# Second norm inside the first gate product, token halves right behind it, 17 pairs by seven, first weight sums in Mamba, down projection behind the last pair

## The chip, the cores and the metric

The kernel runs on one NeuronCore of a Trainium2 chip. The engines that matter are TensorE (PE, matrix products, with its weight loads shown as PEld), VectorE (DVE), ScalarE (ACT), GpSimd (POOL, here almost only for issuing transfers) and SyncE (SP, which issues most loads). Each engine works through its own instructions in order. The metric is the device time of one execution in microseconds. The kernel before was timed three times: 873.16, 873.23 and 875.12 us, median 873.23.

## The reference

The computed layer takes 512 positions of width 1024, with 16 learned positions put ahead of them, in float32. A normalised input goes through one projection to two mixers, their outputs through one output projection, and a gated MLP follows:

```python
def conv_glu_ffn(h, w_up, conv_w, conv_b, w_down):
    u = causal_dwconv(h @ w_up, conv_w, conv_b)
    gate, val = jnp.split(u, 2, axis=-1)
    return (jax.nn.silu(gate) * val) @ w_down

def reference(...):
    h = jnp.concatenate([meta, x], axis=1)
    for l in range(DEPTH):
        u = rmsnorm(h, norm1_w[l])
        proj = u @ w_in[l]
        hg_q, hg_f, hg_i, hg_g, m2_z, m2_xbc, m2_dt = jnp.split(proj, PROJ_SPLITS, axis=-1)
        out_a = hgrn2_mixer(hg_q, hg_f, hg_i, hg_g, lbs[l], hg_norm_w[l])
        out_b = mamba2_mixer(m2_z, m2_xbc, m2_dt, ...)
        h = h + jnp.concatenate([out_a, out_b], axis=-1) @ w_out[l]
        h = h + conv_glu_ffn(rmsnorm(h, norm2_w[l]), ...)
    return rmsnorm(h, final_norm_w)[:, N_META:, :]
```

`rmsnorm` divides by the root of the mean square over the 1024 channels. `w_up` is 1024 x 5632: 2816 gate columns and 2816 value columns. `causal_dwconv` is a convolution of width 3 along the positions, per channel.

## The kernel before

Channels lie on the 128 partitions, positions along the free dimension (528, of which the MLP needs 514). Each float32 operand of a product is split in a high and a low half of a format that TensorE takes (`F32R`), and each product is three matmuls: high by high, high by low, low by high. A weight block of 128 x 1024 is loaded by SP (`raw`), copied by ACT into the high half (`whi`, line 182) and subtracted by DVE for the low half (`wlo`, line 183). There are three buffers of each kind, and blocks are asked for two ahead of their use (`weights`, `ahead`).

The stages in time: input projections with the Mamba mixer between them (to 196 us), the eight HGRN heads, the gate projections, the output projection `pout` (410 to 501 us), the MLP's up projection (to 741 us), its down projection `pdn`, and the final norm.

The output projection leaves `xr`, the new residual, in eight channel blocks. Of each block three things are made: `u2h`/`u2l`, the split block times its norm weight, and the square, added up in `acc`. `second_norm` sums `acc` over the partitions with PE (line 879), and ACT makes `rstd2` of it by Ln and Exp (`log_exp`, lines 140 and 141), two functions that may need a table load each.

The up projection works on 22 pairs of a gate block j and a value block 22 + j. `KINDS` says how each pair is computed:

- **U** (j = 0 to 4): an ordinary product of `u2h`/`u2l`, which are not yet normalised; DVE multiplies the result by `rstd2` afterwards (`fr`, line 963). A pair has 96 matmuls of about half the positions.
- **W** (j = 5 to 20): `scheme(j)`, a product "by seven" in the manner of Strassen and Winograd. The pair's weights and its tokens are seen as 2 x 2 blocks, and seven half products, 84 matmuls, 258 positions wide, do the work of eight. It needs normalised tokens `n` (DVE line 902), combinations `t1` to `t4` of token halves (lines 912 to 915), all of these split by `split_half` (lines 189 and 190), and combinations of weights.
- **N** (j = 21): an ordinary product of the normalised tokens, 96 matmuls.

The combined weights of a W pair (`sums`) are made by transfers alone: `weight_sums` issues, from POOL's queue, copies and accumulating transfers between arrays in device memory, six for each pair, in four groups of pairs. Each group has a gate: DVE copies a value of a tile that is produced at a chosen time (`ticks`), and POOL copies that (`tick`, line 196), so its queue stands until then. `scheme_weights` later loads three weight blocks of each W pair (`w0`, `w2`, `w1`) and a half block `s4`, which is split into `s4h`/`s4l`.

`normed_tokens(i)` makes the tokens in eight steps; `STEPS` says behind which pair each is issued. `SPLITS` says the same of the splits of the gated results `ac` for the down projection. The down projection's first two column blocks (`pdn0`, `pdn1`) go over all 22 blocks of `ac` together.

A scheduler sets the order of each engine's instructions before the launch, by simulated times and by priorities: `first()` and `evac()` raise a priority, and `issue_after` says that an instruction stands in order behind another one. It adds no wait at run time by itself. Engines wait for each other by the data and by the buffers: a new tile in a pool of three waits for the last reader of the tile three before.

## Time and profile before

| | us |
|---|---|
| runs | 873.16, 873.23, 875.12 |
| profiled execution: time, span | 873.16, 871.3 |
| PE busy | 851.0 (98%) |
| DVE busy | 579.6 (67%) |
| ACT busy | 464.1 (53%) |
| POOL busy | 93.7 (11%) |

The profiled execution is itself one of the three runs' fastest; 1.9 us of its time lie outside the span that the trace covers. Busy shares are means over stages, and a stage is read by itself. In a row of a timeline the columns are the start, the duration, engine, line, operation, output and inputs; the brackets at its end give the idle time before it and what it waited for. A matmul's duration there runs from its start to its modelled end, and the next one starts before that, so the pace is read from the starts or from the count in a window.

### The profile page before, as it was taken

The numbers are of one execution on the slowest core, as the hardware profiler recorded it, in microseconds if no ns is written. First come the engines' busy times: TensorE is split into PE (matmuls) and PEld (weight loads), VectorE is DVE, ScalarE is ACT, GpSimd is POOL, SyncE is SP. The second block draws the span as 40 slices with busy tenths as digits, with TensorE's granted clock in tenths as the row PEclk, the third lists the DMA queues.
The fourth block names the chain that finished last, engine by engine and source line by source line (L and its number), as shares of the span: only waits on it lengthen the run. The fifth ranks groups of instructions, "written<-read, shape, count | busy, mean of one in ns | idle before, by whom it ended". The sixth has DMA issues, their size and how long they took to land.

```text
span 871.3 us, 16400 instructions
## 1 busy us (share of the span) xinstructions
PE 851.0 (98%) x6746; PEld 810.3 (93%) x6746; DVE 579.6 (67%) x970; ACT 464.1 (53%) x736; POOL 93.7 (11%) x130
## 2 busy tenths in 40 slices
PE   6999999999999999999999999999999999999995
PEld 6999899999999999999999999889999999888885
DVE  6984978799776766545333359978888886633233
ACT  8638975966445434454222265567666665533231
POOL 1000000003213221202221312100000000000001
PEclk9999999999999999999999999999999999999998
DMA  7234242213989598948998889756555553243312
GB/s 248 93 109 163 78 145 62 76 58 128 240 153 166 208 228 160 180 128 305 222 179 178 279 163 192 178 166 185 182 173 189 177 176 115 68 126 90 91 43 97
DMA packets 51867, 135.00 MB, mean 155 GB/s; under 512 B 5432, under 2 KB 9016, under 8 KB 51792
## 3 DMA queue, kind: packets, MB, share of 16 engines
q1 hardware_dynamic: 33392, 92.60, 33.1%
q0 software_dynamic: 15872, 37.75, 23.1%
q10 hardware_dynamic: 2528, 3.60, 1.3%
q8 instruction: 53, 0.87, 0.4%
q14 instruction: 22, 0.18, 0.1%
HBM read 131.78 MB, written 39.90 MB: 197 GB/s over the span
## 4 chain that ended last, share of the span: by engine, by line
PE 87%; DVE 6%; DMA 2%; ACT 2%; issue 1%; SPq 0%; DVEq 0%; ACTq 0%
PE pj L272 32%; PE pout L272 10%; PE pdn L1054 4%; PE pdn L1055 4%; PE pdn L1053 4%; PE pup L982 3%; PE pup L984 3%; PE pup L983 3%; PE psn L983 2%; PE psn L984 2%; PE psn L982 2%; PE pup L272 1%; DVE fc L931 1%; PE pdn L1068 1%; PE pdn L1067 1%
## 5 line engine op out<-in xcount | busy, mean ns | idle before, releaser
L272 PE MATMUL pj<-u_lo,whi_in 128*128 128x272 f32 (+1 forms) x752 | 156.5, 288 | 0.0
L272 PE MATMUL pj<-u_hi,wlo_in 128*128 128x272 f32 (+1 forms) x752 | 156.1, 286 | 0.0
L272 PE MATMUL pj<-u_hi,whi_in 128*128 128x272 f32 (+1 forms) x752 | 155.3, 287 | 0.0
L272 PEld LDWEIGHTS pj<-u_lo,whi_in 128*128 128x128 f32 x752 | 116.1, 188 | 2.4 <-issue 1.9
L272 PEld LDWEIGHTS pj<-u_hi,wlo_in 128*128 128x128 f32 x752 | 116.4, 189 | 2.0 <-issue 1.9
L272 PEld LDWEIGHTS pj<-u_hi,whi_in 128*128 128x128 f32 x752 | 115.6, 188 | 2.4 <-issue 2.3
L183 DVE TENSOR_TENSOR wlo_in<-raw_in,whi_in 128x1024 fp32r<-128x1024 f32 (+1 forms) x58 | 64.3, 1109 | 55.1 <-ACT whi_in L182 55.0
L182 ACT ACTIVATE whi_in<-raw_in 128x1024 fp32r<-128x1024 f32 (+1 forms) x58 | 56.1, 966 | 64.5 <-PE pj L272 59.2
L182 ACT ACTIVATE whi_w<-raw_w 128x1024 fp32r<-128x1024 f32 x48 | 50.7, 1056 | 22.8 <-PE pup L983 11.5
L183 DVE TENSOR_TENSOR wlo_dn<-raw_dn,whi_dn 128x1024 fp32r<-128x1024 f32 (+1 forms) x24 | 27.2, 1135 | 53.3 <-ACT whi_dn L182 53.3
L183 DVE TENSOR_TENSOR wlo_w<-raw_w,whi_w 128x1024 fp32r<-128x1024 f32 x48 | 58.6, 1221 | 5.5 <-ACT whi_w L182 5.0
L182 ACT ACTIVATE whi_dn<-raw_dn 128x1024 fp32r<-128x1024 f32 (+1 forms) x24 | 23.6, 989 | 69.2 <-PE pdn L1054 53.6
L1054 PE MATMUL pdn<-ac_lo,whi_dn 128*128 128x512 f32 (+1 forms) x154 | 55.9, 363 | 0.0
L1053 PE MATMUL pdn<-ac_hi,whi_dn 128*128 128x512 f32 (+1 forms) x154 | 55.7, 362 | 0.0
L1055 PE MATMUL pdn<-ac_hi,wlo_dn 128*128 128x512 f32 (+1 forms) x154 | 55.6, 361 | 0.0
L182 ACT ACTIVATE whi_out<-raw_out 128x1024 fp32r<-128x1024 f32 x16 | 17.0, 1061 | 55.6 <-PE pout L272 29.9
L183 DVE TENSOR_TENSOR wlo_out<-raw_out,whi_out 128x1024 fp32r<-128x1024 f32 x16 | 19.6, 1226 | 29.8 <-ACT whi_out L182 29.8
L1111 POOL TENSOR_TENSOR ot<-xr,rs 128x256 f32<-128x256 f32 x4 | 3.7, 944 | 311.0 <-ACT rs L1102 311.0
L982 PE MATMUL pup<-n_hi,whi_w 128*128 128x258 f32 x128 | 36.3, 283 | 0.5 <-ACT n_hi L189 0.5
L983 PE MATMUL psn<-t,whi_w 128*128 128x258 f32 x128 | 36.4, 284 | 0.0
L983 PE MATMUL pup<-n_lo,whi_w 128*128 128x258 f32 x128 | 36.2, 283 | 0.0
L982 PE MATMUL psn<-t,whi_w 128*128 128x258 f32 x128 | 36.1, 282 | 0.0
(371 smaller groups left out, 2364.2 us busy)
## 6 DMA issues: line engine op xcount, KB each, us to landing
raw_in<-in_w_in_dram SPq DMA_DIRECT2D x50, 512.0 KB, 5.0
sums<-in_w_up_dram POOLq DMA_DIRECT2D x48, 512.0 KB, 8.2
sums<-in_w_up_dram POOLq DMA_DIRECT2D x32, 256.0 KB, 8.3
raw_out<-in_w_out_dram SPq DMA_DIRECT2D x16, 512.0 KB, 6.7
raw_w<-in_w_up_dram SPq DMA_DIRECT2D x16, 512.0 KB, 3.5
raw_w<-sums SPq DMA_DIRECT2D x16, 512.0 KB, 4.1
raw_dn<-in_w_down_dram SPq DMA_DIRECT2D x16, 512.0 KB, 4.0
raw_up<-in_w_up_dram SPq DMA_DIRECT2D x12, 512.0 KB, 8.3
```

The costliest lines, as they stand in the source:

```text
L182: A.activation(hi[:, d], raw[:, d], AF.Copy)
L183: eng.tensor_tensor(lo[:, d], raw[:, d], hi[:, d].bitcast(F32), ALU.subtract)
L272: PE.matmul(ps[:, O + a0:O + a1], w, x[:, a0:a1], start=s, stop=e)
L931: V.scalar_tensor_tensor(c, at(s), w[2 - s], c, ALU.mult, ALU.add)
L982: PE.matmul(ps, wh, xh, start=first, stop=False, skip_group_check=True)
L983: PE.matmul(ps, wh, xl, start=False, stop=False, skip_group_check=True)
L984: PE.matmul(ps, wl, xh, start=False, stop=k == H - 1, skip_group_check=True)
L1053: PE.matmul(ps, wh, xh, start=k0 + k == 0, stop=False)
L1054: PE.matmul(ps, wh, xl, start=False, stop=False)
L1055: PE.matmul(ps, wl, xh, start=False, stop=k0 + k == KF - 1)
L1067: PE.matmul(ps[:], wh, ah[k0 + k][:], start=k0 + k == 0, stop=False)
L1068: PE.matmul(ps[:], wh, al[k0 + k][:], start=False, stop=False)
```

## The change

1. `KINDS`: pair 21 becomes W. There are 17 W pairs, and the last group of weight sums has five pairs (30 transfers).
2. The groups of weight sums move. The first is gated by `ys[3]`, behind the first half of Mamba's heads; the second by `ys[7]`, where the first was; the third and fourth by the HGRN outputs 3 and 7; none by the output projection. DVE's copy for the gate has a raised priority.
3. In the output projection the square and its sum come ahead of `u2h`/`u2l`, and the table for Ln and Exp is loaded behind the first square.
4. `second_norm` is called inside the first gate product, ahead of its seventh channel block, and the token steps 0 and 1 directly behind this product. The other steps follow behind pairs 0, 1 and 2, where they were behind 1, 2 and 3.
5. Of tokens in the first four channel blocks only the first 258 positions are split. `t1` and `t3`, and `t2` and `t4`, are split together, 516 wide.
6. `SPLITS`: block 8 moves from pair 20 to pair 21. The matmuls of the first two column blocks of the down projection stand in order behind the last matmul of the last pair.

Three places in the order of instructions follow, with the tile's number in each name. The first is ACT at the second norm: `psn` is the sum of squares, `rstd` the result, `whi_up` weights of coming products, `fc` the first convolution. Before:

```order
L182 ACTIVATE whi_up_5998<-raw_up_5997 128x1024
L860 ACTIVATE u2h_5985<-xr_5982,pt 128x514
L866 ACTIVATE hsq_5989<-xr_5982 128x514
L182 ACTIVATE whi_up_6068<-raw_up_6067 128x1024
L140 ACT_TABLE_LOAD
L140 ACTIVATE rstd_5992<-psn_0_6053,eps 128x258
L140 ACTIVATE rstd_5992<-psn_1_6055,eps 128x256
L141 ACT_TABLE_LOAD
L141 ACTIVATE rstd_5992<-rstd_5992 128x514
L929 ACTIVATE fc_6060<-fr_6061,pt 128x512
```

Now:

```order
L182 ACTIVATE whi_up_6006<-raw_up_6005 128x1024
L862 ACTIVATE hsq_5993<-xr_5990 128x514
L870 ACTIVATE u2h_5996<-xr_5990,pt 128x514
L140 ACTIVATE rstd_6000<-psn_0_6049,eps 128x258
L140 ACTIVATE rstd_6000<-psn_1_6051,eps 128x256
L141 ACTIVATE rstd_6000<-rstd_6000 128x514
L182 ACTIVATE whi_up_6102<-raw_up_6101 128x1024
L936 ACTIVATE fc_6094<-fr_6095,pt 128x512
```

The two table loads are gone from between the sum and `rstd`, and the weights `whi_up` of a later product stand behind it.

The second is DVE at the last pair, j = 21: `sv` are its sums of products, `s4l` the low half of its last weights, `wlo_dn_c_k` the low halves of the down projection's weights (column block c, from row block k). Before, from the end of pair 20:

```order
L1015 TENSOR_TENSOR sv20_8692<-s720_8693,pup1_6004 128x258
L183 TENSOR_TENSOR wlo_up_43_8755<-raw_up_43_8753,whi_up_43_8754 128x1024
L1016 TENSOR_TENSOR sv20_8692<-s720_8693,psn2_0_6053 128x258
L183 TENSOR_TENSOR wlo_dn_0_0_8829<-raw_dn_0_0_8827,whi_dn_0_0_8828 128x1024
L931 SCALAR_TENSOR_TENSOR fc20_8694<-pup1_6004,pt_75,fc20_8694 128x512
```

Now, from the end of pair 21:

```order
L1046 TENSOR_TENSOR ac20_8809<-fc42_8687,fc20_8686 128x512
L190 TENSOR_TENSOR ac7_lo_8812<-ac7_7117,ac7_hi_8811 128x512
L1025 TENSOR_TENSOR sv21_8816<-s721_8817,pup0_6011 128x258
L183 TENSOR_TENSOR wlo_dn_1_0_8879<-raw_dn_1_0_8877,whi_dn_1_0_8878 128x1024
L1026 TENSOR_TENSOR sv21_8816<-s721_8817,psn2_0_6049 128x258
L190 TENSOR_TENSOR s4l_21_8830<-s4_21_8823,s4h_21_8829 128x512
L183 TENSOR_TENSOR wlo_dn_0_8_9005<-raw_dn_0_8_9003,whi_dn_0_8_9004 128x1024
```

The split of the last pair's `s4` stands behind weights of the down projection; pair 20's stood well ahead of its `sv20`, and is not among those rows. On ACT it is alike, with `s7` the copy of a product:

```order
L1021 ACTIVATE s721_8817<-p7_21_8815 128x258
L189 ACTIVATE ac9_hi_8947<-ac9_7385 128x512
L182 ACTIVATE whi_dn_1_0_8878<-raw_dn_1_0_8877 128x1024
L189 ACTIVATE s4h_21_8829<-s4_21_8823 128x512
L182 ACTIVATE whi_dn_0_8_9004<-raw_dn_0_8_9003 128x1024
```

`s4h` has `whi_dn_1_0` ahead of it, whose buffer is the one that the second weights (`w2`) of pair 21 hold.

The third is POOL in Mamba; `sc1` and `bP1` are tiles of the second HGRN head that POOL fills with zeros. Now, the end of the first group:

```order
L216 DMA sums8_1008<-in_w_up_dram 128x512
L218 DMA sums5_1005<-sums5_1005 128x512
L218 DMA sums6_1006<-sums6_1006 128x512
L218 DMA sums7_1007<-sums7_1007 128x512
L218 DMA sums8_1008<-sums8_1008 128x512
L669 MEMSET sc1_2225 128x512
```

Both memsets stood ahead of the first group before; now `bP1` stands behind 13 of its 24 transfers and `sc1` behind all of them.

The diff:

```diff
--- before.py
+++ after.py
@@ -48,9 +48,9 @@

-KINDS = "UUUUUWWWWWWWWWWWWWWWWN"
-STEPS = {0: (0, 1), 1: (2, 3), 2: (4, 5), 3: (6, 7)}
-SPLITS = {7: (0,), 8: (1, 2), 10: (3,), 13: (4,), 15: (5,), 18: (6,), 20: (7, 8), 21: range(9, 22)}
+KINDS = "UUUUUWWWWWWWWWWWWWWWWW"
+STEPS = {0: (2, 3), 1: (4, 5), 2: (6, 7)}
+SPLITS = {7: (0,), 8: (1, 2), 10: (3,), 13: (4,), 15: (5,), 18: (6,), 20: (7,), 21: range(8, 22)}
 WS = [j for j in range(KF) if KINDS[j] == "W"]
 GROUPS = WS[0:4], WS[4:8], WS[8:12], WS[12:]
 HT = 258
@@ -192,7 +192,8 @@
     def weight_sums(js, behind):

         n = GROUPS.index(js)
-        V.tensor_copy(ticks[:, n:n + 1], behind[:, T0:T0 + 1])
+        with first():
+            V.tensor_copy(ticks[:, n:n + 1], behind[:, T0:T0 + 1])
         gate = G.tensor_copy(tick[:], ticks[:, n:n + 1])
         halves = w_up.rearrange("(a j) p c -> j p a c", a=2)
         ds = {}
@@ -260,10 +261,12 @@
         ahead(used[0] + 2)
         return wdone.pop(key)

-    def product(groups, xh, xl, t0, nk, k0=0):
+    def product(groups, xh, xl, t0, nk, k0=0, calls={}):


         for k in range(len(xh)):
+            if k in calls:
+                calls[k]()
             first, last = k0 + k == 0, k0 + k == nk - 1
             for ps, (hi, lo) in groups:
                 wh, wl = hi[:, k * P:(k + 1) * P], lo[:, k * P:(k + 1) * P]
@@ -635,6 +638,7 @@
     mamba_states(0)
     next_phase(LOGS)
     mamba_heads(0)
+    weight_sums(GROUPS[0], ys[3])
     load_ab(1)
     mamba_gates(0)
     next_phase(SILU)
@@ -678,7 +682,7 @@
         return ap.rearrange("p (a t) -> p a t", t=n)[:, :, lo:lo + n // 2].rearrange("p a (c t) -> p a c t", t=16)

     os_ = []
-    weight_sums(GROUPS[0], ys[7])
+    weight_sums(GROUPS[1], ys[7])

     def hgrn_head(h):
         i = h % 2
@@ -822,7 +826,7 @@
         hgrn_head(h)
         if h % 4 == 3:
             hgrn_norm(h - 3)
-            weight_sums(GROUPS[1 + h // 4], os_[h])
+            weight_sums(GROUPS[2 + h // 4], os_[h])
     oah, oal = [], []
     for h in range(NH):
         o = os_[h]
@@ -854,20 +858,20 @@
         V.tensor_tensor(xr[:, T0:], xr[:, T0:], pos[j][:, O + T0:O + NT], ALU.add)
         dump(f"h{j}", xr[:])
         hs.append(xr)
-        if j == 5:
-            weight_sums(GROUPS[3], xr)
+        sq = slot(f"hsq{j}", tag="pr")
+        square = A.activation(sq[:, T0:], xr[:, T0:], AF.Square)
+        if acc is None:
+            acc = sq
+            with tc.issue_after(square.ins):
+                A.preload_act_table_set(LOGS)
+        else:
+            V.tensor_tensor(acc[:, T0:], acc[:, T0:], sq[:, T0:], ALU.add)
         hi, lo = slot(f"u2h{j}", dtype=F32R, tag="u"), slot(f"u2l{j}", dtype=F32R, tag="u")
         A.activation(hi[:, T0:], xr[:, T0:], AF.Copy, scale=col(C_N2 + j))
         V.scalar_tensor_tensor(lo[:, T0:], xr[:, T0:], col(C_N2 + j), hi[:, T0:].bitcast(F32),
                                ALU.mult, ALU.subtract)
         u2h.append(hi)
         u2l.append(lo)
-        sq = slot(f"hsq{j}", tag="pr")
-        A.activation(sq[:, T0:], xr[:, T0:], AF.Square)
-        if acc is None:
-            acc = sq
-        else:
-            V.tensor_tensor(acc[:, T0:], acc[:, T0:], sq[:, T0:], ALU.add)
     rstd2 = slot("rstd2", tag="rs")

     u1 = []
@@ -902,22 +906,25 @@
                 V.scalar_tensor_tensor(t[:, T0:], hs[kk][:, T0:], col(C_N2 + kk), rstd2[:, T0:], ALU.mult, ALU.mult)
                 tag = "b0" if kk % 4 < 2 else "b1"
                 hi, lo = slot(f"n{kk}_hi", dtype=F32R, tag=tag), slot(f"n{kk}_lo", dtype=F32R, tag=tag)
-                split_half(t[:, T0:], hi[:, T0:], lo[:, T0:])
+                d = slice(T0, NT) if kk >= KD // 2 else tails[0]
+                split_half(t[:, d], hi[:, d], lo[:, d])
                 nh[kk], nl[kk] = hi, lo
                 fs[k] += [t[:, c] for c in tails]
             return
         b11, b12, b21, b22 = fs[k]
-        t13, t24 = slot(f"t13_{k}", tag="ab"), slot(f"t24_{k}", tag="ab")
+        t13, t24 = slot(f"t13_{k}", 2 * HT, tag="ab"), slot(f"t24_{k}", 2 * HT, tag="ab")
         t1, t3, t2, t4 = t13[:, 0:HT], t13[:, HT:2 * HT], t24[:, 0:HT], t24[:, HT:2 * HT]
         V.tensor_tensor(t1, b11, b12, ALU.subtract)
         V.scalar_tensor_tensor(t2, b22, -1.0, t1, ALU.mult, ALU.subtract)
         V.tensor_tensor(t3, b22, b12, ALU.subtract)
         V.scalar_tensor_tensor(t4, t2, -1.0, b21, ALU.mult, ALU.subtract)
-        ts.append([])
-        for n, t in enumerate((t1, t2, t3, t4)):
-            d = slot(f"t{n + 1}_{k}", 2 * HT, F32R)
-            split_half(t, d[:, 0:HT], d[:, HT:])
-            ts[-1].append((d[:, 0:HT], d[:, HT:]))
+        ts.append([None] * 4)
+        for n, t in enumerate((t13, t24)):
+            hi, lo = (slot(f"t{n}{x}_{k}", 2 * HT, F32R) for x in "hl")
+            split_half(t[:], hi[:], lo[:])
+            for i in range(2):
+                d = slice(i * HT, (i + 1) * HT)
+                ts[-1][n + 2 * i] = hi[:, d], lo[:, d]

     def taps(c, r, j, w, b):

@@ -950,11 +957,12 @@
         w = weights("up", j)
         ps = product_banks(False)[0]
         if kind == "U":
-            product([(ps, w)], u2h, u2l, T0, KD)
+            product([(ps, w)], u2h, u2l, T0, KD, calls={6: second_norm} if j == 0 else {})
         else:
             product([(ps, w)], nh, nl, T0, KD)
         if j == 0:
-            second_norm()
+            for i in (0, 1):
+                normed_tokens(i)
         r = ps[:, O + T0:O + NT]
         c = slot(f"fc{j}", 512, tag="pr")
         with evac():
@@ -965,6 +973,8 @@
             taps(c[:], r, j, taps_of(j), col(C_FB + j))
         return c

+    last_product = []
+
     def scheme(j):

         xz, was = product_banks(True)
@@ -981,7 +991,7 @@
                 first = start and k == 0
                 PE.matmul(ps, wh, xh, start=first, stop=False, skip_group_check=True)
                 PE.matmul(ps, wh, xl, start=False, stop=False, skip_group_check=True)
-                PE.matmul(ps, wl, xh, start=False, stop=k == H - 1, skip_group_check=True)
+                last_product[:] = [PE.matmul(ps, wl, xh, start=False, stop=k == H - 1, skip_group_check=True)]

         def seed(ps, of):

@@ -1061,12 +1071,13 @@
     pdn = [bank(f"pdn{j}") for j in range(2)]
     for k0, kc in PARTS:
         w2 = [weights("dn", j, k0) for j in range(2)]
-        for k in range(kc):
-            for ps, (hi, lo) in zip(pdn, w2):
-                wh, wl = hi[:, k * P:(k + 1) * P], lo[:, k * P:(k + 1) * P]
-                PE.matmul(ps[:], wh, ah[k0 + k][:], start=k0 + k == 0, stop=False)
-                PE.matmul(ps[:], wh, al[k0 + k][:], start=False, stop=False)
-                PE.matmul(ps[:], wl, ah[k0 + k][:], start=False, stop=k0 + k == KF - 1)
+        with tc.issue_after(last_product[0].ins):
+            for k in range(kc):
+                for ps, (hi, lo) in zip(pdn, w2):
+                    wh, wl = hi[:, k * P:(k + 1) * P], lo[:, k * P:(k + 1) * P]
+                    PE.matmul(ps[:], wh, ah[k0 + k][:], start=k0 + k == 0, stop=False)
+                    PE.matmul(ps[:], wh, al[k0 + k][:], start=False, stop=False)
+                    PE.matmul(ps[:], wl, ah[k0 + k][:], start=False, stop=k0 + k == KF - 1)
     for j in range(KD):
         if j > 1:
             ws = [(weights("dn", j, k0), k0, kc) for k0, kc in PARTS]
```

## The prediction

> **What bounds the kernel now.** I read the page's first section, then the busy time by stage, then the stretches of TensorE (PE) where the two disagree. The page says one engine is the kernel:
>
> ```profile
> PE 851.0 (98%) x6746; PEld 810.3 (93%) x6746; DVE 579.6 (67%) x970; ACT 464.1 (53%) x736; POOL 93.7 (11%) x130
> ```
>
> By stage (columns: window, its length, busy time and instructions of PE, weight load, DVE, ACT and POOL, granted clock, DMA share, GB/s):
>
> ```profile
> 118.00:190.00 72.00, 72.00 (x632) 66.95 (x631) 59.63 (x102) 53.83 (x98) 1.30 (x2) 1.00 0.24 77
> 208.00:278.00 70.00, 70.00 (x620) 68.17 (x619) 49.23 (x119) 29.25 (x48) 22.12 (x25) 1.00 0.88 197
> 393.00:470.00 77.00, 77.00 (x650) 77.00 (x649) 31.94 (x39) 25.03 (x32) 20.27 (x25) 1.00 0.94 231
> 501.00:559.00 58.00, 58.00 (x487) 57.89 (x486) 49.23 (x80) 34.02 (x50) 12.71 (x14) 1.00 0.92 183
> ...
> 576.00:721.00 145.00, 145.00 (x1209) 145.00 (x1208) 122.34 (x165) 100.94 (x152) 0.00 (x0) 1.00 0.58 182
> ...
> 558.91:576.01 17.10, 13.22 (x100) 12.12 (x98) 14.90 (x25) 10.82 (x19) 0.00 (x0) 1.00 0.42 131
> ```
>
> PE is full in Mamba (118 to 190), in the first HGRN heads, in the output projection, in the U products and in the pairs by seven. The stretch from 576 also gives the price of a half-width matmul: 145.00/1209 = 0.120 us. (The 283 ns that the page shows for one is its time from start to end; they overlap.) The only hole inside is the first pair by seven, at 558.91: 97 of the window's 100 rows (three reach in from its ends) at 0.120 are 11.6 us and it took 17.1, so it **loses 5.4 us**. All five stops in it, from PE's timeline:
>
> ```profile
> 561.03 0.39 PE L982 MATMUL pup<-n_hi,whi_w 128*128 128x258 f32 x1 [0.53 <-ACT n_hi L189]
> 562.16 0.39 PE L984 MATMUL p<-t,wlo_w 128*128 128x258 f32 x1 [0.74 <-DVE wlo_w L183]
> 564.06 0.39 PE L1003 MATMUL pup<-n_hi,whi_w 128*128 128x258 f32 x1 [0.46 <-ACT psn L989]
> 567.98 0.39 PE L983 MATMUL p<-t,whi_w 128*128 128x258 f32 x1 [0.49 <-DVE t L190]
> 570.37 0.39 PE L982 MATMUL pup<-t,whi_w 128*128 128x258 f32 x1 [1.65 <-ACT pup L989]
> ```
>
> The waits add to 3.9 us; the rest is a slower restart behind each (some 0.1 us apiece, as 0.39 beside 0.28 shows) and pitches that the wait records miss. Everything in the change is therefore worth only what it does to PE's count, to this hole, or to a new one.
>
> **One pair fewer in the old form.** The pair j = 21 had 96 matmuls, in the chain 0.119 us each:
>
> ```profile
> 728.23 3.80 PE pup L272 x32
> ```
>
> 96 x 0.119 = 11.42 us become 84 x 0.120 = 10.08: **-1.34 us**. This term is firm to 0.1.
>
> **The first pair by seven.** Its operands hang on the second norm (timelines of ACT and DVE):
>
> ```profile
> 508.00 1.28 ACT L140 ACT_TABLE_LOAD   x1
> 510.15 1.28 ACT L141 ACT_TABLE_LOAD   x1
> 511.45 0.64 ACT L141 ACTIVATE rstd<-rstd 128x514 f32<-128x514 f32 x1
> 512.12 0.69 DVE L963 TENSOR_TENSOR fr<-pup,rstd 128x514 f32<-128x514 f32 x1 [2.87 <-ACT rstd L141]
> ```
>
> PE now does the norm 7 matmuls earlier (0.8 us), and both table loads leave the path, the one table being fetched in the output projection, where ACT is busy 25.03 of 77 us. Without 1.28 + 1.28 and the 0.8, less what overlapped, rstd2 is done at about 508.9 and not 512.09: 3.2 us earlier. DVE is the engine that runs behind it. Its groups from 512 to 569 (count, sum in us, mean ns):
>
> ```profile
> L931 DVE SCALAR_TENSOR_TENSOR fc<-fr,pt,fc 128x512 f32<-128x512 f32 x20 | 14.9, 747 | 1.0 <-ACT fc L929 0.9
> L183 DVE TENSOR_TENSOR wlo_up<-raw_up,whi_up 128x1024 fp32r<-128x1024 f32 x6 | 7.3, 1221 | 1.0 <-ACT whi_up L182 1.0
> L963 DVE TENSOR_TENSOR fr<-pup,rstd 128x514 f32<-128x514 f32 x10 | 6.9, 688 | 2.9 <-ACT rstd L141 2.9
> L190 DVE TENSOR_TENSOR t<-t,t 128x258 fp32r<-128x258 f32 x16 | 6.4, 421 | 0.0
> L902 DVE SCALAR_TENSOR_TENSOR n<-xr,pt,rstd 128x514 f32<-128x514 f32 x8 | 5.7, 748 | 0.0
> L190 DVE TENSOR_TENSOR n_lo<-n,n_hi 128x514 fp32r<-128x514 f32 x8 | 5.4, 687 | 0.0
> L183 DVE TENSOR_TENSOR wlo_w<-raw_w,whi_w 128x1024 fp32r<-128x1024 f32 x4 | 4.9, 1218 | 0.0
> L1036 DVE TENSOR_TENSOR ac<-fc,fc 128x512 f32<-128x512 f32 x5 | 3.4, 685 | 0.0
> L912 DVE TENSOR_TENSOR t<-n 128x258 f32<-128x258 f32 x4 | 1.7, 421 | 0.0
> ...
> 512.12:568.18 56.06, 53.83 (x443) 52.93 (x443) 53.99 (x92) 33.77 (x53) 10.70 (x12) 1.00 0.85 173
> ```
>
> With the three other t steps (1.7 each) these are 62 us of durations in 54 us of busy time: neighbours overlap, by a factor of 0.87. In the new order DVE has, from the first fr up to the low half of the first pair's last weights, 9 fr, 16 fc, 8 n, 9 wlo, 16 t of 258, 4 n_lo of 258 and 4 of 514, 7 t splits of 516 (as 0.687 for 514), 3 ac and one s4l: 6.2 + 12.0 + 6.0 + 11.0 + 6.7 + 1.7 + 2.7 + 4.8 + 2.1 + 0.7 = 53.9, times 0.87 = 46.9. From 508.9 that ends at 555.8, or 557.9 with the 2.1 us that DVE idled before. Those last weights cannot be split sooner anyway, since their buffer is freed by the last U product:
>
> ```profile
> 558.87 1.06 ACT L182 ACTIVATE whi_w<-raw_w 128x1024 fp32r<-128x1024 f32 x1 [0.87 <-PE pup L272]
> 560.88 1.22 DVE L183 TENSOR_TENSOR wlo_w<-raw_w,whi_w 128x1024 fp32r<-128x1024 f32 x1
> 569.95 0.37 ACT L989 ACTIVATE pup<-psn 128x258 f32<-128x258 f32 x1
> ```
>
> So DVE is no longer late, and two stops stay. First the weights: ACT 558.87 to 559.93, DVE to 561.21, while the third matmul on t3 (PE's 15th of the pair) would start at 558.91 + 14 x 0.12 = 560.59: 0.7 us. Second the seed that ACT copies between two banks: the last matmul before it needs its 0.28, the copy 0.37, and PE has nothing between: about 0.6. With a restart of 0.1 each, 1.5 us stay and **-3.9 us** are won. Bounds: 0, if DVE's place behind another wait keeps it late, and -5.4, if nothing stays.
>
> **The last pair.** In the old order the products of j = 21 and 16 down matmuls lay between the parts of pair 20, and pair 20's last weights h4 were long ready:
>
> ```profile
> 707.47 0.63 ACT L189 ACTIVATE s4h<-s 128x512 fp32r<-128x512 f32 x1 [0.95 <-PE pup L983]
> ...
> 726.61 0.29 PE L982 MATMUL pup<-n_hi,s4h 128*128 128x258 f32 x1
> ...
> 723.87 1.06 ACT L182 ACTIVATE whi_up<-raw_up 128x1024 fp32r<-128x1024 f32 x1 [1.48 <-PE pup L983]
> 724.96 1.23 DVE L183 TENSOR_TENSOR wlo_up<-raw_up,whi_up 128x1024 fp32r<-128x1024 f32 x1 [0.53 <-ACT whi_up L182]
> ```
>
> Pair 21 has nothing behind it that may fill in: the down products are held behind its last product. And its s4h stands on ACT behind whi_dn_1_0, which waits until the t1 product ends and frees a buffer (as 723.87 did for the same buffer of pair 20). Call that end E. whi_dn_1_0 runs to E + 1.2, s4h to E + 1.7; DVE has wlo_dn_1_0 (1.23) and sv21 (0.42) ahead of s4l, which ends at E + 3.4. PE reaches h4's first low-half matmul after 12 on t4 and two more, at E + 1.7. It stands 1.8 us, with a restart **+1.9 us**. Bounds: 0, if ACT and DVE get to s4 sooner; +3.5, if the transfer of s4, issued behind three down weights, lands 1.6 us later than I have it. The held matmuls only move: their number is the same. The split of ac8 moves behind pair 21 too; it is first needed by the 49th down matmul, and the down projection had no stop there before.
>
> **The sums in Mamba.** The first group of 24 accumulating transfers now starts when ys[3] is done, and not at 207.60:
>
> ```profile
> 115.68 0.74 DVE L581 SCALAR_TENSOR_TENSOR cv<-cv,pt,psy 128x512 f32<-128x512 f32 x1
> 174.71 0.75 POOL L665 MEMSET sc<- 128x512 f32 x1 [43.53 <-DVE ab L559]
> 207.60 2.93 POOL L196 COPY tick<-ticks 128x1 f32<-128x1 f32 x1 [32.14 <-DVE ticks L195]
> 277.64 0.81 POOL L217 DMA_DIRECT2D sums<-sums  x1 [1.35 <-issue]
> 224.39 0.73 DVE L782 COPY_PREDICATED sc<-maskA,pa 128x512 f32<-128x512 int32 x1
> ```
>
> One group holds POOL's queue 277.64 + 0.81 - 207.60 = 70.9 us, so it runs from 117 to 188. Behind it on POOL now stands the memset of the second sc (0.75 us), which DVE first needs at 224.39: 36 us of slack. DMA share is 0.24 there, so there is room. The other groups only move forward, and the U stage loses their traffic. **0 us**; the bound above is rival D.
>
> **Sum.** -1.34 - 3.9 + 1.9 = -3.3 us on a span of 871.3; with the 1.9 us that this execution (873.16) has around its span, 869.8. It stands 0.07 below the median, 873.23.
>
> **Rivals.** *A, the sum, 869.8*: 0.53, its own range 868.9 to 870.7. *B, the last pair does not stop*: if the low half of s4 gets ahead of the down weights, 873.2 - 1.3 - 3.9 = 867.9, and 866.4 if the first pair's stops vanish as well. For it: s4h of pair 20 was ready 19 us early; against: the written order of ACT puts it behind a wait. 0.18. *C, the first pair keeps its stops*: DVE is busy 122.34 of 145 us in the pairs and 53.99 of 56.06 ahead of them, so a gap anywhere may eat the 3 us of lead. At half the gain 871.8, at none 873.7. 0.22. *D, slower*: POOL's transfers slow down in Mamba where DVE is busier. If they progress only while DVE is idle, a group of 20.8 idle us in 70 (208 to 278) needs 70.9 x (20.8/70)/(12.4/72) = 122 us and ends at 239; the memset of sc then comes 14 us after 224.4, DVE stands there in order with all that PE waits for, and the time is about 869.8 + 14 = 884. It decides from 107 us on. Against it, another group, with the last of its 24 transfers issued at 468.6 and its first in the window from 393, took as long with DVE busy 31.94 of 77. 0.07.
>
> ```profile
> L217 POOL DMA_DIRECT2D sums<-sums x4: 812/818/837, 458.6 to 468.6; - x4
> ```
>
>  The Trainium skill (page "SBUF — State Buffer", section "SBUF: two separate sides") states such a lock: descriptors of transfers issued on POOL's queue cannot be written while DVE runs a two-port copy. By that rule the group would stretch in Mamba; the two group times above, alike under unlike DVE loads, do not bear it out here.
>
> **How the numbers follow.** 0.3% of 873.23 is 2.6 us, about what a measurement can tell from no change: faster is below 870.6. All of B and nearly all of A lie there (0.68), C between (0.25), D above (0.07). The range 866.8 to 872.6 takes A, nearly all of B, and C up to three quarters of the lost gain; outside are D, the end of C and the end of B.
>
> **What would show it.** rstd2's Exp ends near 509, first fr behind it, no table load between. The first pair by seven loses about 1.5 us, at a wlo_w and at a seed. One PE stop of about 1.8 us before the down projection, released by the split of s4. Mamba stays at 100% of PE, with sums transfers from 117 to about 190, and the down projection has no new stop. I am wrong if the first pair still stops for n or t splits, if s4 is early, or if PE waits in the first HGRN heads.

## The result, and the profile after

The changed kernel takes 869.36 us (median of 4, 869.19 to 869.76) against 873.59 beside it (the three runs above and a fourth, 873.95); the ratio, which is not simply the quotient of the two medians, is 0.9949, 95% interval 0.9932 to 0.9966. That is half a per cent faster, and 0.4 us below the 869.8 that was predicted. One execution of ten of tokens_late, below, took 2136.59 us and counts in no ratio. The profiled execution has a span of 867.4 us, 3.9 less than before. TensorE is as full as it was; from the page of the changed kernel:

```profile
PE 848.9 (98%) x6734; PEld 808.8 (93%) x6734; DVE 579.8 (67%) x966; ACT 463.1 (53%) x732; POOL 97.2 (11%) x136
```

The stretches that answer to those shown of before, with the same columns. Mamba (118 to 190) is full although the DMA share there went from 0.24 to 0.87; in the 17 us from the first matmul of the first pair by seven, at 558.83, 133 matmuls fit where 100 did:

```profile
118.00:190.00 72.00, 72.00 (x631) 66.95 (x630) 59.78 (x102) 53.50 (x98) 19.18 (x24) 1.00 0.87 201
...
573.00:718.00 145.00, 145.00 (x1209) 145.00 (x1208) 123.03 (x166) 100.36 (x152) 0.00 (x0) 1.00 0.57 181
...
558.80:576.00 17.20, 16.37 (x133) 15.93 (x132) 14.51 (x20) 12.14 (x19) 0.00 (x0) 1.00 0.51 151
```

Four stops are left in the up projection, and they are those that the prediction named, the last one in two parts. TensorE's timeline of the changed kernel, the first pair and the last:

```profile
561.22 0.39 PE L994 MATMUL p<-t0h,wlo_w 128*128 128x258 f32 x1 [0.55 <-DVE wlo_w L183]
566.28 0.39 PE L992 MATMUL pup<-t0h,whi_w 128*128 128x258 f32 x1 [0.28 <-ACT pup L999]
731.00 0.39 PE L992 MATMUL pup<-n_hi,s4h 128*128 128x258 f32 x1 [0.16 <-ACT s4h L189]
732.68 0.39 PE L994 MATMUL pup<-n_hi,s4l 128*128 128x258 f32 x1 [1.17 <-DVE s4l L190]
```

From start to start they cost more than the bracket says: 561.22 follows a matmul at 560.39, so 0.83 - 0.12 = 0.71 us; the others 0.44, 0.32 and 1.33. With some 0.1 us of slow restart behind each, the first pair loses 1.4 us (5.4 before), the last one 1.85. Ahead of the last pair's `s4h` on ACT, and of its `s4l` on DVE, stand weights of the down projection:

```profile
729.37 1.06 ACT L182 ACTIVATE whi_dn<-raw_dn 128x1024 fp32r<-128x1024 f32 x1 [0.46 <-ACT ac_hi L189]
730.34 0.61 ACT L189 ACTIVATE s4h<-s 128x512 fp32r<-128x512 f32 x1
...
730.46 1.23 DVE L183 TENSOR_TENSOR wlo_dn<-raw_dn,whi_dn 128x1024 fp32r<-128x1024 f32 x1 [0.52 <-ACT whi_dn L182]
731.61 0.42 DVE L1026 TENSOR_TENSOR sv<-s,psn 128x258 f32<-128x258 f32 x1
731.94 0.68 DVE L190 TENSOR_TENSOR s4l<-s,s4h 128x512 fp32r<-128x512 f32 x1
```

The second norm, on ACT and then DVE:

```profile
506.87 0.91 ACT L140 ACTIVATE rstd<-psn,eps 128x258 f32<-128x258 f32 x2 [3.78 <-PE psn L883]
507.80 0.64 ACT L141 ACTIVATE rstd<-rstd 128x514 f32<-128x514 f32 x1
...
508.47 0.69 DVE L971 TENSOR_TENSOR fr<-pup,rstd 128x514 f32<-128x514 f32 x1 [3.99 <-ACT rstd L141]
```

rstd2 is ready at 508.44, 3.65 us earlier than before. And POOL's queue in Mamba, from the gate to the memset that stands behind the first group:

```profile
116.23 0.18 POOL L197 COPY tick<-ticks 128x1 f32<-128x1 f32 x1 [8.50 <-DVE ticks L196]
188.76 0.81 POOL L218 DMA_DIRECT2D sums<-sums  x1 [2.09 <-issue]
189.28 0.83 POOL L669 MEMSET sc<- 128x512 f32 x1
```

The group takes 73.3 us and not 70.9, and `sc1` is ready 34 us before its first use. TensorE has one stop in the HGRN heads, at 296 us behind the norm of the first four; it is 0.90 us long and was 0.43. The first projection had started 0.47 us earlier (25.37 and not 25.84), which is lost there, and in the chain of waits the output projection starts 0.1 us earlier. Before, and now:

```profile
410.01 91.12 PE pout L272 x768
```

```profile
409.92 91.12 PE pout L275 x768
```

So nearly all of the 3.9 us in the span lie behind the U products. From the start of their last row in TensorE's timeline (558.67 before, 558.59 now) to the start of the last sum of squares (862.56 and 858.84) it is 303.89 us before and 300.25 now, 3.64 less. This part of the execution is called the late part below. The count of matmuls, the first pair and the last pair make -1.34 - 4.0 + 1.85 = -3.5 us of it.

### The profile page after: what moved, and what is told of

Its sections match the earlier page's. It is cut to its first block, busy times and chain, and to the rows that moved or that the text cites. A ratio compares the mean times of both kernels' runs of the same rounds, so it can differ in the third digit from the quotient of the medians.

```text
span 867.4 us, 16403 instructions
## 1 busy us (share of the span) xinstructions
PE 848.9 (98%) x6734; PEld 808.8 (93%) x6734; DVE 579.8 (67%) x966; ACT 463.1 (53%) x732; POOL 97.2 (11%) x136
## 4 chain that ended last, share of the span: by engine, by line
PE 93%; ACT 2%; DMA 2%; DVE 1%; issue 1%; SPq 0%; DVEq 0%
PE pj L275 32%; PE pout L275 11%; PE pup L275 6%; PE pup L994 4%; PE pup L992 4%; PE pup L993 4%; PE pdn L1064 4%; PE pdn L1065 4%; PE pdn L1063 4%; PE psn L993 2%; PE psn L994 2%; PE psn L992 2%; PE pdn L1078 1%; PE pdn L1080 1%; PE pdn L1079 1%; PE psy L575 1%
## 5 line engine op out<-in xcount | busy, mean ns | idle before, releaser
L182 ACT ACTIVATE whi_w<-raw_w 128x1024 fp32r<-128x1024 f32 x51 | 53.9, 1057 | 26.9 <-PE pup L993 11.7
L183 DVE TENSOR_TENSOR wlo_w<-raw_w,whi_w 128x1024 fp32r<-128x1024 f32 x51 | 62.3, 1221 | 8.5 <-ACT whi_w L182 8.0
L992 PE MATMUL pup<-n_hi,whi_w 128*128 128x258 f32 x136 | 38.6, 284 | 0.0
L993 PE MATMUL psn<-t1l,whi_w 128*128 128x258 f32 x136 | 38.6, 284 | 0.0
L994 PE MATMUL psn<-t1h,wlo_w 128*128 128x258 f32 x136 | 38.4, 283 | 0.0
L993 PE MATMUL pup<-n_lo,whi_w 128*128 128x258 f32 x136 | 38.4, 282 | 0.0
```

Source lines behind the costliest of these rows:

```text
L182: A.activation(hi[:, d], raw[:, d], AF.Copy)
L183: eng.tensor_tensor(lo[:, d], raw[:, d], hi[:, d].bitcast(F32), ALU.subtract)
L992: PE.matmul(ps, wh, xh, start=first, stop=False, skip_group_check=True)
L993: PE.matmul(ps, wh, xl, start=False, stop=False, skip_group_check=True)
L994: last_product[:] = [PE.matmul(ps, wl, xh, start=False, stop=k == H - 1, skip_group_check=True)]
```

## The experiments

All are edits of the changed kernel, but for tokens_alone, which edits the kernel before. The table has medians, the ratio to the kernel before beside it, and the late part's time in the one profiled execution of each. The kernel before alone has medians from 873.19 to 873.65 beside these runs, and many of the intervals overlap, so a median a few tenths off another shows nothing by itself. The late part leaves out the scatter of the start and of the end:

| kernel | us | ratio, 95% interval | late part, us |
|---|---|---|---|
| before | 873.59 | | 303.89 |
| changed | 869.36 | 0.9949 [0.9932, 0.9966] | 300.25 |
| t2_first | 869.78 | 0.9956 [0.9943, 0.9970] | 300.10 |
| t2_ac7 | 867.27 | 0.9930 [0.9917, 0.9942] | 298.30 |
| last_ordinary | 869.90 | 0.9957 [0.9945, 0.9970] | 300.04 |
| no_hold | 869.14 | 0.9950 [0.9938, 0.9962] | 299.98 |
| ac7_behind | 867.69 | 0.9935 [0.9922, 0.9947] | 298.44 |
| w1_early_ac7 | 866.92 | 0.9929 [0.9916, 0.9941] | 297.59 |
| tokens_late | 872.55 | 0.9990 [0.9981, 0.9999] | 303.34 |
| norm_old | 869.76 | 0.9964 [0.9951, 0.9977] | 300.37 |
| widths_old | 869.95 | 0.9958 [0.9943, 0.9972] | 300.53 |
| sums_old | 873.27 | 0.9998 [0.9986, 1.0010] | 303.67 |
| sums_old_5first | 879.51 | 1.0072 [1.0058, 1.0085] | 300.24 |
| tokens_alone | 870.18 | 0.9961 [0.9947, 0.9974] | 299.49 |

### What wins the first pair

**tokens_late** puts the token steps back.

```diff
-STEPS = {0: (2, 3), 1: (4, 5), 2: (6, 7)}
+STEPS = {0: (0, 1), 1: (2, 3), 2: (4, 5), 3: (6, 7)}
...
-        if j == 0:
-            for i in (0, 1):
-                normed_tokens(i)
```

> The changed kernel with the token steps behind pairs 0, 1, 2 and 3 again, instead of the first behind the first gate product and the others behind pairs 0, 1 and 2. The second norm stays early. By the order, DVE makes the last tokens of the fourth step only behind the last U product's result: 14 of its instructions, with wlo of w1 and w0 among them, stand between that and the low half of t2, some 9.6 us, while TensorE would use it 5.7 us into the first pair. My theory: it is the place of the tokens, not the norm's 3.2 us, that wins most of the first pair: stops of 4 us, 869.4 + 2.9 = 872.3. Rival (as the prediction had it): the lead of DVE comes from the norm 3.2 us earlier and the 2.3 us less of splitting, and the same instructions are done by then in whatever order: 869.4, at most 870.

872.55 us: 3.2 us of the change's gain are gone (3.1 in the late part), as the theory had it, but no stop is for the low half of t2, where the theory looked. TensorE's waits (in total, times, longest) in the first pairs by seven are again for weights and seeds that stand behind token work:

```profile
PE pup L1010 <- ACT psn L996: 1.1, 2, 0.6
PE p L991 <- DVE wlo_w L183: 0.9, 1, 0.9
...
PE pup L989 <- ACT pup L996: 0.5, 1, 0.5
PE pup L991 <- DVE wlo_w L183: 0.4, 1, 0.4
```

**norm_old** undoes the early norm alone.

```diff
-        sq = slot(f"hsq{j}", tag="pr")
-        square = A.activation(sq[:, T0:], xr[:, T0:], AF.Square)
...
-            with tc.issue_after(square.ins):
-                A.preload_act_table_set(LOGS)
...
         u2l.append(lo)
+        sq = slot(f"hsq{j}", tag="pr")
+        square = A.activation(sq[:, T0:], xr[:, T0:], AF.Square)
...
-            product([(ps, w)], u2h, u2l, T0, KD, calls={6: second_norm} if j == 0 else {})
+            product([(ps, w)], u2h, u2l, T0, KD, calls={})
...
         if j == 0:
+            second_norm()
```

> The changed kernel with the square and its sum behind u2h and u2l, no table load in the output projection and the second norm called behind the first gate product, all as before; the tokens stay where the change put them. rstd2 is then 3.2 us later, by the table loads and seven matmuls. DVE idled 2.3 us ahead of the low half of w1 in the changed kernel, so it is 0.9 us late there, and the order of the first pair's product on t3 is broken up. My theory: +0.5 to +1.2, 870.2. Rival: all of the first pair's gain hangs on the early norm, which is what the old order's DVE waited for at its start: 869.4 + 3.2 = 872.6.

869.76: rstd2 3.4 us later (done at 511.83 and not 508.44) costs 0.4 us by the medians, which their scatter does not tell from nothing, and 0.1 in the late part; that is less than the theory had, and nothing like the rival's 3.2. The stop for w1 is replaced by one for the first seed (0.8 us), the other one stays:

```profile
PE pup L1012 <- ACT psn L998: 0.8, 1, 0.8
...
PE pup L991 <- ACT pup L998: 0.3, 1, 0.3
```

The call inside the product moves nothing by itself: with `second_norm` behind the product and the rest of the change left in, the instructions of all five engines stand in the same order as in the changed kernel. TensorE's norm seven matmuls earlier thus comes from the place of the square and of the table load.

**widths_old** splits all tokens over all positions, and t1 to t4 one by one.

```diff
-                d = slice(T0, NT) if kk >= KD // 2 else tails[0]
+                d = slice(T0, NT)
...
-        for n, t in enumerate((t13, t24)):
+        for n, t in enumerate((t1, t2, t3, t4)):
```

> The changed kernel with the splits as before: all eight token blocks over all positions, and t1 to t4 split one by one, 258 wide. DVE and ACT then have 2.0 us more each of splitting ahead of the first pair by seven, DVE against 2.3 us of idle time there. By the order, two matmuls of the product on t3 now stand ahead of the product on b11, where they wait for the high half of w1 (ready at 559.9, some 1.0 us after the last U product). My theory: the wider splits win little by themselves, since the spare time covers them; what is lost is that displacement, some 1.0 us less the 0.8 that this wait then saves later, and a wait for a seed of up to 0.6: 869.4 + 0.7 = 870.1. Rival: DVE's time is what the pair waits for, and 2.0 us come back in full: 871.4.

869.95, the theory within 0.2 (it is 0.6 more than the changed kernel, 0.3 in the late part). The wait is where the theory put it, for the high half of w1 and then for a seed:

```profile
PE p L990 <- ACT whi_w L182: 0.9, 1, 0.9
...
PE pup L1011 <- ACT psn L997: 0.5, 1, 0.5
```

**tokens_alone** makes the tokens' place the only change to the kernel before.

```diff
-STEPS = {0: (0, 1), 1: (2, 3), 2: (4, 5), 3: (6, 7)}
+STEPS = {0: (2, 3), 1: (4, 5), 2: (6, 7)}
...
         if j == 0:
             second_norm()
+            for i in (0, 1):
+                normed_tokens(i)
```

> The kernel before with one part of the change: the token steps 0 and 1 behind the first gate product, the others behind pairs 0, 1 and 2. Norm, tables, splits, sums and the last pair are as before. Undone one at a time, the tokens' place cost 3.2 us, the early norm 0.4 and the narrow splits 0.6. My theory: the last two were cheap only because each used up the same 2.3 us in which DVE idles ahead of the low half of w1 in the changed kernel. Here both are missing: rstd2 comes 3.7 us later and DVE splits 2.0 us more, 5.7 us against 2.3, so w1 is 3.4 us late, the first pair loses some 4.3 us and not 5.4, and the time is 873.2 - 1.1 = 872.1. Rival: the parts add, and the tokens' place alone wins its 2.9 of the 3.9 us: 870.3.

870.18: 3.0 us won, the rival, and the theory of a shared 2.3 us falls. The five executions lie apart, from 868.75 to 870.64; the traced one is at 869.02, and in it the late part is 4.4 us shorter than before. What the slower ones lose, no trace shows. Three rows of the traced one show why: the window from the first `fr` to the first pair by seven, DVE's row for the low half of w1, and the only wait of TensorE's list that lies in the up projection:

```profile
512.00:558.00 46.00, 46.00 (x390) 46.00 (x389) 45.64 (x79) 27.47 (x43) 10.67 (x12) 1.00 0.90 184
```

```profile
560.98 1.22 DVE L183 TENSOR_TENSOR wlo_w<-raw_w,whi_w 128x1024 fp32r<-128x1024 f32 x1
```

```profile
PE pup L1005 <- ACT psn L991: 0.5, 1, 0.5
```

With the norm late DVE idles 0.4 us in 46. The changed kernel has, up to 558 and then ahead of the low half of w1:

```profile
508.50:558.00 49.50, 49.50 (x418) 49.50 (x417) 47.79 (x77) 27.32 (x39) 0.00 (x0) 1.00 0.33 100
...
559.93 1.23 DVE L183 TENSOR_TENSOR wlo_w<-raw_w,whi_w 128x1024 fp32r<-128x1024 f32 x1 [2.31 <-ACT whi_w L182]
```

There DVE idles 1.7 us to 558 and 1.9 from there to 559.93, together 3.6: the time it has no work for is about the whole lead of the norm, and not only the 2.3 us ahead of w1. The low half of w1 starts at 560.98, 1.05 us later than in the changed kernel (559.93) and not 3.4: I had counted everything ahead of it in the changed kernel's order, and this order puts some of it behind. By the starts, only 0.8 us of stops are left in its first pair.

### The stops that the change leaves

**t2_first** turns two products of the first pair round.

```diff
         mul(y, w2h[:, 0:HK], w2l[:, 0:HK], t2)
+        t2_last = last_product[0]
...
+        with ExitStack() as st:
+            if j == WS[0]:
+                st.enter_context(tc.issue_after(t2_last.ins))
+            mul(v, w1h[:, 0:HK], w1l[:, 0:HK], t3, True)
```

> The changed kernel with one edit: in the first pair by seven, TensorE's product on t2 stands in order ahead of the product on t3 (behind it before). Nothing else is meant to move. My theory: the two stops that are left in this pair (0.71 us for the low half of the weights w1, 0.44 us for the seed that ACT copies, and about 0.1 us of slow restart behind each) are a matter of order alone: with t2 first, the weights have 2.9 us more, and the copy is covered by the 1.44 us product on t3. The pair loses nothing, and the time is 869.4 - 1.3 = 868.1. Rival: DVE is still too late here, so the product on t2 stops for the last low half of t2 (made from 561.68 to 562.37 in the changed kernel) or for its weights; a new stop of the same size takes the old ones' place and the time stays 869.4.

869.78: nothing won. Both old stops are gone and one of 1.2 us is new, but neither t2 nor its weights cause it. TensorE's row, and ACT's rows ahead of it:

```profile
561.73 0.39 PE L1013 MATMUL pup<-n_hi,whi_w 128*128 128x258 f32 x1 [1.02 <-ACT psn L999]
```

```profile
559.12 1.06 ACT L182 ACTIVATE whi_w<-raw_w 128x1024 fp32r<-128x1024 f32 x1 [3.13 <-issue]
560.09 0.62 ACT L189 ACTIVATE t1h<-t 128x516 fp32r<-128x516 f32 x1
560.61 0.80 ACT L936 ACTIVATE fc<-fr,pt 128x512 f32<-128x512 f32 x1
561.32 0.36 ACT L999 ACTIVATE psn<-pup 128x258 f32<-128x258 f32 x1
```

The next product adds to the bank of which ACT must first copy a seed, and that copy stands behind three other instructions of ACT. The product on t3 had covered it.

**t2_ac7** adds the split of block 7 behind pair 21:

```diff
-... 18: (6,), 20: (7,), 21: range(8, 22)}
+... 18: (6,), 21: range(7, 22)}
```

> As t2_first, and the split of gated block 7 moves from behind pair 20 to behind pair 21, so that it no longer holds two of the five buffers in which s4, s4h and s4l of the last pair are made. My theory: the last pair's stop (0.32 us for s4h and 1.33 us for s4l, 1.85 us with restarts) comes from this: without the two buffers s4 is loaded and split a pair earlier, as for all other pairs, and 868.1 - 1.85 = 866.2. Rival: what PE waited for moves on: the down projection then starts 1.9 us earlier, and its second weight block dn_1_0, which no change makes faster, or the low half of block 7 stops it by as much; 868.1.

**last_ordinary** is t2_first with the last pair as before.

```diff
-KINDS = "UUUUUWWWWWWWWWWWWWWWWW"
+KINDS = "UUUUUWWWWWWWWWWWWWWWWN"
...
-... 20: (7,), 21: range(8, 22)}
+... 20: (7, 8), 21: range(9, 22)}
...
-                d = slice(T0, NT) if kk >= KD // 2 else tails[0]
+                d = slice(T0, NT)
...
-        with tc.issue_after(last_product[0].ins):
+        with ExitStack() as _:
```

> As t2_first, with the last pair in the old form (96 matmuls), the splits of blocks 7 and 8 behind pair 20 and no hold on the down projection, as before the change; the tokens of the first four channel blocks are split over all positions, since the old form needs them (1.1 us more on DVE before the first pair by seven). My theory: the seven products save 1.34 us of matmuls there and cost 1.85 us of stop, so undoing the last pair alone makes it faster: 868.1 + 1.34 - 1.85 = 867.6. Rival: PE's number of matmuls decides, and undoing it costs 1.3 us: 869.4.

Times: 867.27 and 869.90. The first pair differs between them, so the stretch behind it decides, from the restart at L1013 to the last sum of squares at the end, in TensorE's timelines. t2_first runs from 561.73, above, to 858.98; t2_ac7 follows, then last_ordinary:

```profile
858.98 0.70 PE L1115 MATMUL psn<-fsq,cf 128*128 128x256 f32 x2 [0.96 <-ACT fsq L1111]
```

```profile
561.23 0.39 PE L1013 MATMUL pup<-n_hi,whi_w 128*128 128x258 f32 x1 [1.02 <-ACT psn L999]
...
856.67 0.70 PE L1115 MATMUL psn<-fsq,cf 128*128 128x256 f32 x2 [0.96 <-ACT fsq L1111]
```

```profile
562.35 0.39 PE L1013 MATMUL pup<-n_hi,whi_w 128*128 128x258 f32 x1 [1.54 <-ACT psn L999]
...
859.01 0.70 PE L1115 MATMUL psn<-fsq,cf 128*128 128x256 f32 x2 [0.96 <-ACT fsq L1111]
```

That is 297.25, 295.44 and 296.66 us. So the last pair by seven with its stop is 0.6 us slower than in the old form (theory: 0.5), and without the stop 1.2 us faster (1.34 by the count of matmuls). last_ordinary's whole time is no better than t2_first's, since its first pair stops 0.5 us longer. The stop was a matter of five buffers, of which block 7's two halves held two: the next experiment, which moves only that split, has the load of the last `s4` issued 18 us earlier.

**ac7_behind** is that one edit on the changed kernel, **w1_early_ac7** the same with the first pair's w1 ahead of w2:

```diff
-            chunks += [((w, j), None, KD) for w in ("w0", "w2", "w1")]
+            chunks += [((w, j), None, KD) for w in (("w0", "w1", "w2") if KINDS[j - 1] == "U" else ("w0", "w2", "w1"))]
```

> The changed kernel with one edit: the split of gated block 7 stands behind pair 21 and not behind pair 20. With t2_first the same edit took away the whole last stop. My theory: it does so alone, 1.85 us, and the down projection does not stop in its place: 869.4 - 1.85 = 867.5, with the first pair's two stops (0.71 and 0.44 us) as in the changed kernel. Rival: what t2_ac7 won beyond 1.85 us (869.8 to 867.3 is 2.5) came from the edit too, in the down projection: 866.9.

> As ac7_behind, and for the first pair by seven alone the weights w1 are loaded and split ahead of w2 (behind them before), so that w1 has the buffer that an earlier U product frees 11 us before and w2 waits for the last U product. TensorE's order is the same. My theory: w2 is needed first by the product on t2, which starts 4.5 us into the pair, and its split ends 2.4 us into it, so the stop for w1 (0.71 us and 0.1 of restart) goes and nothing comes in its place; the seed's 0.44 us stay: 867.5 - 0.8 = 866.7. Rival: PE, 0.8 us ahead, waits as much longer for ACT's two copies between banks (the seeds), as in t2_first, where a stop of 1.2 us for the first of them took the place of both: 867.5.

867.69 and 866.92, both as the theory had it (867.5, 866.7): in the late part the two edits win 1.81 and 0.85 us. The last is the fastest kernel here, 0.71% under the one before. The load of the last pair's `s4`, in SP's timelines of the changed kernel and of ac7_behind:

```profile
723.77 0.38 SPq L233 DMA_DIRECT2D s<-sums  x1
```

```profile
705.30 0.32 SPq L233 DMA_DIRECT2D s<-sums  x1
```

Of the up projection's stops, the waits of w1_early_ac7 show one:

```profile
PE pup L992 <- ACT pup L999: 0.3, 1, 0.3
```

**no_hold** lets the down products into the last pair.

```diff
-        with tc.issue_after(last_product[0].ins):
+        with ExitStack() as _:
```

> The changed kernel without the hold on the down projection: its matmuls may stand in order inside the last pair. 20 matmuls of the first column block and two of the second (0.233 us each) come to stand ahead of the last pair's h4 product, 2 of them ahead of the product on t1. My theory: they fill the stop for s4h and s4l, since weights dn_0_0 are ready 3 us before it, and they are only moved: 869.4 - 1.85 = 867.5. Rival: the hold is what keeps the last pair on time: with 4.6 us of down matmuls ahead of h4, the last gated block and the split of later blocks come as much later and the down projection stops for them: 869.4 or more.

869.14, 0.2 us less (0.3 in the late part): the rival's mechanism, if not its time. No stop is left for s4, and new ones stand in the down projection, for splits of `ac` and for weights that now come too late, and take back most of it:

```profile
PE pdn L1079 <- DVE ac_lo L190: 0.7, 2, 0.5
...
PE pdn L1080 <- DVE wlo_dn L183: 0.2, 1, 0.2
```

### Where the sums may stand

**sums_old** gates the four groups as before.

```diff
-    weight_sums(GROUPS[0], ys[3])
...
-    weight_sums(GROUPS[1], ys[7])
+    weight_sums(GROUPS[0], ys[7])
...
-            weight_sums(GROUPS[2 + h // 4], os_[h])
+            weight_sums(GROUPS[1 + h // 4], os_[h])
...
+        if j == 5:
+            weight_sums(GROUPS[3], xr)
```

> The changed kernel with the four groups of weight sums gated as before: by ys[7], the HGRN outputs 3 and 7, and the sixth residual block. TensorE's order is the same. The sums' transfers then lie in the output projection and the U products again, and Mamba has none. My theory: no stop hangs on them, neither in Mamba (TensorE is at 100% with and without) nor in the U products (weights are asked for two blocks ahead, and the median landing of 8.3 us before against 3.5 us after is hidden either way): 869.4, within 0.4. Rival: the U products' weights land late enough for DVE and ACT to be late at the first pair by seven, and part of its gain comes from the sums leaving the U products: its stops grow by 1 us or more, 870.4 or more.

873.27: the whole gain is gone, more than even the rival asked. In this order its timelines of POOL (the last issue of the sums), of ACT (s4h of pair 6, and what it waited for) and of TensorE (the stop), and the window behind the stop, in which TensorE is full at a granted clock of 0.50:

```profile
567.91 0.83 POOL L218 DMA_DIRECT2D sums<-sums  x1 [0.59 <-issue]
```

```profile
565.51 0.63 ACT L189 ACTIVATE s4h<-s 128x512 fp32r<-128x512 f32 x1 [3.60 <-DMA s<-sums]
```

```profile
568.11 0.38 PE L993 MATMUL pup<-n_hi,whi_w 128*128 128x258 f32 x1 [1.93 <-ACT whi_w L182]
```

```profile
569.00:570.00 1.00, 1.00 (x5) 1.00 (x6) 0.99 (x2) 0.00 (x0) 0.00 (x0) 0.50 0.88 193
```

The last group has 30 transfers now and runs on into the first pair by seven. What stops TensorE are weights of pair 6, which stand on ACT behind the split of that pair's late `s4`; the rival had put it down to weights of the U products.

**sums_old_5first** keeps those places and makes the first group the one of five pairs.

```diff
-GROUPS = WS[0:4], WS[4:8], WS[8:12], WS[12:]
+GROUPS = WS[0:5], WS[5:9], WS[9:13], WS[13:]
```

> As sums_old, gated at the same four places, but the group of five pairs is the first (behind ys[7]) and the last (behind the sixth residual block) has four, as it had before the change. The order of all engines is that of sums_old but for POOL's queue. In sums_old the last group's 30 transfers ran from 480 to 568.7 us, 17 us longer than the 24 did before, past the first pair by seven, where s4 of pair 6 landed 9 us after its issue and ACT stood for it with the weights of pair 6 queued behind. My theory: the fifth pair in the last group is what costs; with four the transfers end near 552, before the weights of pairs 5 and 6 are loaded, and the time is that of the changed kernel, 869.4. Rival: any sums in the U products slow the weights and cost there: 871 to 873.3, as sums_old.

879.51, neither. From the first pair by seven on the theory holds: its stops are the changed kernel's two again, and the late part takes as long as the changed kernel's (300.24 and 300.25 us). But in the HGRN heads the stop of 0.9 us has become one of 9.4, and TensorE loses some 1.6 us more behind it, at a granted clock of 0.50. TensorE's wait, POOL's last issue of the first group, and DVE's row that was waited for in turn:

```profile
PE pm L796 <- DVE mt L783: 9.4, 1, 9.4
```

```profile
294.36 0.81 POOL L218 DMA_DIRECT2D sums<-sums  x1 [0.47 <-issue]
...
303.13 0.75 DVE L822 SCALAR_TENSOR_TENSOR o<-o,pt,rb 128x514 f32<-128x514 f32 x1 [4.65 <-DMA rb<-rs_d]
```

The norm of the first four heads sends rows to device memory and back to all partitions (`rb`); with sums still under way it ends at 303.9 and not at 295.1, and `mt` stands on DVE behind it. So the fifth pair has to go somewhere, and of the old places neither the first nor the last holds it; the two between were not tried.

## Why the prediction was right, step by step

- **The count of matmuls, -1.34.** Right: 1.2 by t2_ac7 against last_ordinary.
- **The last pair, +1.9.** Right, 1.85, by the named instructions in the named order: s4h and s4l behind weights of the down projection (0.32 of the stop is for s4h already, where I had it all at s4l). What I did not see is why they stood there. Pair 20's were early and pair 21's were not because the splits of block 7 held two of five buffers, and moving one number removes the stop.
- **The first pair, -3.9.** Right in size: it loses 1.4 us and I had 1.5 (0.71 for w1, as forecast; the seed 0.44, not 0.6). The step that failed is the cause: "Its operands hang on the second norm". I took DVE's lead from rstd2 being 3.2 us earlier and only counted the new order along with it. The runs say: the tokens' place alone wins 3.0 us (4.4 in the late part, more than the first pair's 4.0), and undoing it loses 3.2 (3.1); undoing the norm loses 0.4 (0.1) and undoing the narrow splits 0.6 (0.3). The norm's lead of 3.65 us (3.2 forecast) was there, and ended as idle time of DVE. That the size came out all the same is partly luck: I worked it out from the stops that stay, and the change happened to move the tokens too. By my reasoning tokens_late, with the norm as early, would have kept the gain. Rival C, half the gain for lack of lead on DVE, had the same wrong picture.
- **The sums, 0.** Right against the kernel before, and rival D is refuted in this place: 73.3 us for a group with DVE busy 59.78 of 72, against 70.9 with 49.23 of 70 and, for the group from 393.34 in the kernel before, 76.1 with 31.94 of 77. The Trainium skill (page "SBUF — State Buffer", section "SBUF: two separate sides") lets transfers of POOL's queue starve behind DVE's two-port copies, where rival D counted all of DVE's work; the trace shows 2.4 us of that at most. But my reading that the other groups "only move forward" at no price and no gain left out what the move is for: with five pairs in it, the last group in its old place costs 3.9 us (3.4 in the late part). That is part of the price of the seventeenth pair, and the sum was right only because the change pays it in Mamba, where nothing waits.
- **Range and chances.** 869.36 lies in the likeliest case's own range (868.9 to 870.7), and the stops that the traces show are that case's. The gain itself is 4.2 us against the 3.4 of the forecast (873.23 to 869.8); 0.36 of the difference is the kernel before, whose median beside the changed one is 873.59.

## What to carry to other kernels

Where an in-order engine runs late, ask first in which order it does its work, and only then how much work there is and when its first operand comes: here the place of eight steps won 3 us or more and a lead of 3.65 us on their input nearly nothing. A stop removed by turning work round can uncover the wait that the old order had hidden (t2_first, no_hold), so read what the moved piece had been covering; the two edits that won beyond the change were ones that had a buffer earlier. The background transfers here cost nothing until a short round trip through memory or a just-in-time load met them, so place them by where they end, not by where they start.

## What the runs showed of the hardware

In sums_old TensorE stood 2.1 us, ran two matmuls and stood another 0.5, and the granted clock was then 0.50 from about 568.5 to 571.9, with 0.215 us from matmul to matmul and not 0.12: some 1.4 us on top of the stop. In the kernel before, five stops of 0.6 to 1.8 us within 10 us left the clock at 1.00. And with the accumulating transfers under way weight loads of 512 KB landed after 7.4 us and of 256 KB after 8.0 (medians, 540 to 575 in sums_old), where they took 3.4 and 3.6 in the changed kernel.
